# A hybrid decoder block on one core: compressed-branch probabilities stacked, gate weights as one stationary, fewer products for sums

## The chip, the cores and the metric

The kernel runs on one core of one Trainium2 chip. The metric is the device time of one execution in microseconds; of several executions the median is taken. Work is issued to five engines, each with its own instruction queue: TensorE (PE in the profile; PEld is its weight load), VectorE (DVE), ScalarE (ACT), GpSimd (POOL) and SyncE (SP, which here only issues DMA transfers).

## The reference

One layer on x of 256 rows by 1024 columns, with 256 memory rows. All inputs and outputs are fp32. Cut to the parts around the change:

```python
h = rmsnorm(x, g_pre_mix)
z = h @ w_in            # q, six k/v, gates, mLSTM inputs, q_mem, merge gates
# compressed branch: blocks of 32 rows, stride 16 -> 15 compressed keys and values
kc, vc = compress_blocks(k, ...), compress_blocks(v, ...)
s = einsum('bsghd,bngd->bghsn', q, kc) * NSA_SCALE
p = masked_softmax(s, end <= t)
o_cmp = einsum('bghsn,bngd->bsghd', p, vc)
# selected and window branches have the same q; with 256 rows both are causal softmaxes
gb = sigmoid(g_nsa)     # three gates a head: 48 columns of z
y_nsa = gb0 * o_cmp + gb1 * o_slc + gb2 * o_win
# mLSTM: 4 + 4 gate columns of z, a running sum of log-sigmoid over the rows, a running maximum
b = cumsum(logf); m_t = running maximum; ...
# memory cross-attention, merge of three projections, w_out, SwiGLU feed-forward of 2816
```

There are 4 groups of 4 query heads of 64 columns. rmsnorm needs the sum of squares of each row of x and of mem.

## The kernel before

**Precision.** A product of fp32 matrices is made of products of high and low parts: `split(hi, lo, src)` copies src to a rounded type on ACT (`hi`), and VectorE subtracts (`lo = src - hi`). A full product is hi·hi + lo·hi + hi·lo (`mm3`, `fmaj`, `tmaj`): three TensorE instructions for each 128-row step of the contraction. Weights come from HBM as units of 128 x 1024 (512 KB): the tile `raw` (four buffers) is filled by a DMA, `whi` (ACT) and `wlo` (VectorE) are made of it, four buffers each. Small products, such as sums by a column of ones, run in plain fp32.

**Stages.** First the keys and values of the memory: `memt` (mem, transposed, in pieces of two or one 128-row blocks) is scaled to `mh`, `ml`, and multiplied with the units of `mem_k` (0 to 3, the first three fetched in halves) and `mem_v`, while `xt` (x transposed, two DMAs of 512 KB) arrives. The sums of squares go through `colsum`: a product of the squares with a column of ones, one for each of two row halves `j` and two column halves `tb`. POOL raises them to the power -0.5, `bcast` spreads them, and VectorE and ACT make `xt` scaled, `hh` and `hl` (the parts of h).

Then the k/v units for the compressed branch ("kv" 0 to 3): `pd` goes to `st` (ACT and VectorE copies), `ph` is the first layer of the compression (32 products of 75 columns in fp32, two blocks of 16), `hid` its result. `w1` (two transfers of 1 MB) reuses the buffers of `memt`, `mh`, `ml`. `mraw` (masks, 208 KB) is issued behind it and cast to `msk`. The gates (`pgf`) are 56 columns of w_in: the host pads them to 128 columns (`wg`), `gw` holds the parts, and `fmaj` makes 8 x 3 products. `gts` is a copy, `pg` its transpose, `og` and `logf` follow. `pf` is the running sum (`tri` is a triangle of ones), `cm` the running maximum (eight VectorE steps on 4 x 256), `nm` its negative, `pm` brings it back to rows. `hrep` repeats the hidden values of the compressed v along the columns, so that the product `pvc` stands at every row block where it is wanted; `vcs` holds its high and low parts side by side (64 + 64 columns).

**Attention stage.** For 4 groups x 2 row halves, `nsa_half(g, tb, qs, yT)`: scores `sc`, maximum `mx`, exponentials `pp` (selected and window) and `pc` (compressed, 16 of 32 columns a head, the rest zero), scaled by the gates over the sums (`sm`). Then transposes `ptn` and `ptc`, parts `pTh`, `pTl` and `ch`, `cl`, and products into `pvn`, which holds the high part of v's columns on 64 partitions and the low part on the other 64. For the compressed branch the 128 rows of `ch` are 4 heads x 32; POOL multiplies with the mask `bm` to make `ce`, in which each head has its own 128 columns and zeros in the rows of the other heads, so that one stationary serves all heads. Other work (units of the mLSTM and of the merge gates) is called in between by `fill`.

Then projections, w_out, feed-forward.

**Order of instructions.** All operations are first recorded (`Plan.record`; hence nearly every row of the profile has the same line, L511, and tiles tell them apart). `Plan.choose` then lists them with a model of durations, dependences and buffers, tries variants of that list by a seeded random search, and issues the best in one fixed order per engine. Any change in an operation's size or number starts another search.

Of the kernel before, what the change touches and what calls it, by code (L numbers as in the profile page):

```python
# [11 lines left out]
F32 = mybir.dt.float32  # L12
# [502 lines left out]
def block_kernel(ctx, tc, order, xN, xT, memT, cst, vec, row, wg, w1, w2, W, out):  # L515
# [42 lines left out]
    def split(hi, lo, src):  # L558
        ACT.activation(hi, src, AF.Copy)
        DVE.tensor_sub(lo, src, hi.bitcast(F32))  # L560
# [95 lines left out]
    def colsum(sq):  # L656

        col = ps_t([P, 2], "col")
        for j in range(2):
            for tb in range(2):  # L660
                PE.matmul(col[:, tb:tb + 1], sq[:, j, tb * P:(tb + 1) * P], ones[:, 0:1],
                          start=j == 0 and tb == 0, stop=j == 1, skip_group_check=True)
        return col

    def bcast(r, ps):
# [35 lines left out]
        split(kmem[:, 0, 2 * i:2 * i + 2, :], kmem[:, 1, 2 * i:2 * i + 2, :], kt)  # L701

    rw = one.tile([P, 520], F32, name="rw")
    wgt = work.tile([P, 1024], F32, tag="p", bufs=2, name="wgt")
    w2t = one.tile([P, 192], F32, name="w2t")
    dma(out=vc, in_=vec)
    warm_up(10)
# [104 lines left out]


    pgf = ps_s([P, S], "pgf")
    gw = [wpool.tile([P, 1024], F32R, tag=t, bufs=4, name="gw") for t in ("whi", "wlo")]
    split(gw[0], gw[1], wgt)
    fmaj(pgf, X, range(KD), gw)
    gts = work.tile([64, S], F32, tag="sq", bufs=3, name="gts")
    DVE.tensor_copy(gts, pgf[0:64])
    pg = ps_s([P, 2, 64], "pg")  # L820
    for tb in range(2):
        PE.transpose(pg[:, tb, :], gts[:, tb * P:(tb + 1) * P], cs[0:64, K_ID:K_ID + 64])
# [15 lines left out]

    tri = cs[:, K_TRI:K_TRI + P]
    pf = ps_t([P, 2, 4], "pf")  # L840
    PE.matmul(pf[:, 0, :], tri, logf[:, 0, :], start=True, stop=True)
    PE.matmul(pf[:, 1, :], ones, logf[:, 0, :], start=True, stop=False)
    PE.matmul(pf[:, 1, :], tri, logf[:, 1, :], start=False, stop=True)
    Fs = one.tile([P, 2, 4], F32, name="Fs")
    DVE.tensor_copy(Fs, pf)
    As = one.tile([P, 2, 4], F32, name="As")
# [21 lines left out]
    DVE.tensor_add(idr, ident[:, 0:4], ident[:, 32:36])  # L868
    pm = ps_t([P, 2, 4], "pm")
    for tb in range(2):  # L870
        PE.matmul(pm[:, tb, :], nm[:, tb * P:(tb + 1) * P], cs[0:4, K_ID:K_ID + 4], start=True, stop=True)
    nmf = work.tile([P, 2, 4], F32, tag="g4", bufs=4, name="nmf")
    DVE.tensor_sub(nmf, pm, Fs)
    em = one.tile([P, 2, 4], F32, name="em")
# [9 lines left out]
    PE.matmul(pk, w2t[:, 0:P], hid[:, 0, :, 0:16], start=True, stop=True)  # L884
    split(kh[:, :, 256:272], kl[:, :, 256:272], pk)
    pvc = ps_t([P, NG, 64], "pvc")
    hrep = work.tile([P, NG, 4, 32], F32, tag="sq", bufs=3, name="hrep")
    POOL.tensor_tensor(hrep, hid[:, 1, :, :].unsqueeze(2).to_broadcast([P, NG, 4, 32]),
                       ones[:, 0:32].unsqueeze(1).unsqueeze(1).to_broadcast([P, NG, 4, 32]), op=ALU.mult)
    for g in range(NG):  # L890
        PE.matmul(pvc[:, g, :], hrep[:, g, :, :], w2t[:, P:192], start=True, stop=True)
    split(vcs[:, :, 0:64], vcs[:, :, 64:128], pvc)
# [188 lines left out]
    ynh = bigt("Y", 2, [P, 8, S], F32R, "ynh")  # L1081
    ynl = bigt("Y", 2, [P, 8, S], F32R, "ynl")
    exps = []
    pcs = [one.tile([P, HPG, 32], F32, name=f"pc{i}") for i in range(2)]
    for t in pcs:
        POOL.memset(t, 0.0)
    bm = cs[:, K_BM:K_BM + 4]
    rvalid = cs[:, K_RV:K_RV + 1]

    def nsa_half(g, tb, qs, yT):  # L1090
        t = slice(tb * P, (tb + 1) * P)
        pc = pcs[tb]
        pv = ps_v([P, HPG, P], "pvn")
        nkb = tb + 1
        for pr in range(2):
            mx = work.tile([P, 2, 3], F32, tag="mx", bufs=3, name="mx")
            sm = work.tile([P, 2, 3], F32, tag="sm", bufs=3, name="sm")
            pp = work.tile([P, 1024], F32, tag="p", bufs=2, name="pp")
            pv4 = pp[:, 0:512 * nkb].rearrange("p (h b n) -> p h b n", h=2, b=2)
            for j in range(2):  # L1100
                q = qs[:, 2 * pr + j, t]
                if tb == 0:
                    s = ps_s([P, 512], "sc")
                    PE.matmul(s[:, 0:272], q, kh[:, g, P:400], start=True, stop=False)
                    PE.matmul(s[:, 0:272], q, kl[:, g, P:400], start=False, stop=False)
                    PE.matmul(s[:, 0:272], identb, M0, start=False, stop=True)
                    sc = (s[:, P:144], s[:, 0:P], s[:, 144:272])
                else:
                    s, s2 = ps_s([P, 512], "sc"), ps_s([P, 512], "sc")
                    for x, c, n in ((s, 0, 272), (s2, 272, 256)):  # L1110
                        PE.matmul(x[:, 0:n], q, kh[:, g, c:c + n], start=True, stop=False, skip_group_check=True)
                        PE.matmul(x[:, 0:n], q, kl[:, g, c:c + n], start=False, stop=False, skip_group_check=True)
                    PE.matmul(s[:, 0:P], identb, MD, start=False, stop=False, skip_group_check=True)
                    PE.matmul(s[:, 256:272], identb, MC1, start=False, stop=True, skip_group_check=True)
                    PE.matmul(s2[:, P:256], identb, MD, start=False, stop=True, skip_group_check=True)
                    sc = (s[:, 256:272], s[:, 0:256], s2[:, 0:256])
                for b in range(3):
                    DVE.tensor_reduce(mx[:, j, b:b + 1], sc[b], axis=AX.X, op=ALU.max, negate=True)
                for b in range(3):
                    out = pc[:, 2 * pr + j, 0:16] if b == 0 else pv4[:, j, b - 1]  # L1120
                    exps.append(ACT.activation(out, sc[b], AF.Exp, bias=mx[:, j, b:b + 1],
                                               accum_out=sm[:, j, b:b + 1]))
            h0 = HPG * g + 2 * pr
            DVE.tensor_mul(sm, sm, og[:, tb, 3 * h0:3 * h0 + 6].rearrange("p (h b) -> p h b", h=2))
            DVE.reciprocal(sm, sm)
            if tb == 0:
                DVE.tensor_scalar(sm[:, :, 0], sm[:, :, 0], rvalid, None, op0=ALU.mult)
            for j in range(2):
                for b in range(3):
                    o = pc[:, 2 * pr + j, 0:16] if b == 0 else pv4[:, j, b - 1]  # L1130
                    DVE.tensor_scalar(o, o, sm[:, j, b:b + 1], None, op0=ALU.mult)
            for kb in range(nkb):
                pt = ps_t([P, 2, 2, P], "ptn")
                for b in range(2):
                    for j in range(2):
                        n = kb if b or not tb else 1 - kb
                        PE.transpose(pt[:, b, j, :], pv4[:, j, b, n * P:(n + 1) * P], ident)
                th = work.tile([P, 512], F32R, tag="pT0", bufs=2, name="pTh")
                tl = work.tile([P, 512], F32R, tag="pT1", bufs=2, name="pTl")
                split(th, tl, pt.rearrange("p a b c -> p (a b c)"))  # L1140
                for b in range(2):
                    for i, x in enumerate((th, tl)):
                        PE.matmul(pv[:, 2 * pr:2 * pr + 2, :], vs[:, kb, b, g, :], x[:, 256 * b:256 * b + 256],
                                  start=(pr == 0 and kb == 0 and b == 0 and i == 0), stop=False,
                                  skip_group_check=True)
        pt = ps_t([P, P], "ptc")
        PE.transpose(pt, pc.rearrange("p h n -> p (h n)"), ident)
        cl = work.tile([P, P], F32, tag="cl", bufs=1, name="cl")
        ch = work.tile([P, P], F32R, tag="ch", bufs=1, name="ch")
        ACT.activation(ch, pt, AF.Copy)  # L1150
        DVE.tensor_sub(cl, pt, ch.bitcast(F32))
        ce = [work.tile([P, HPG, P], F32R, tag=f"ce{i}", bufs=1, name=f"ce{i}") for i in range(2)]
        for i, x in enumerate((ch.bitcast(F32), cl)):
            POOL.tensor_tensor(ce[i], x.unsqueeze(1).to_broadcast([P, HPG, P]),
                               bm.unsqueeze(2).to_broadcast([P, HPG, P]), op=ALU.mult)
        for pr in range(2):
            for i in range(2):
                PE.matmul(pv[:, 2 * pr:2 * pr + 2, :], vcs[:, g, :], ce[i][:, 2 * pr:2 * pr + 2, :],
                          start=False, stop=(pr == 1 and i == 1), skip_group_check=True)
        ylo = work.tile([64, HPG, P], F32, tag="sq", bufs=3, name="ylo")  # L1160
        ACT.activation(ylo, pv[64:128], AF.Copy)
        for e in range(2):
# [163 lines left out]
def _layout(inputs):  # L1326
# [10 lines left out]
    def blocks(w, cols, k0=0, k1=None):  # L1337

        k1 = w.shape[0] // P if k1 is None else k1
        return w[k0 * P:k1 * P, cols].reshape(k1 - k0, P, -1).transpose(1, 0, 2)  # L1340
# [41 lines left out]
        pe("cmp_pe_k"), pe("cmp_pe_v")], axis=1)  # L1382
    w2 = np.concatenate([w2k, w2k, a["cmp_w2_v"][0]], axis=1)
    row = np.concatenate([a[n] for n in ("ml_head_g", "ml_gate_b", "g_post_mix", "g_post_ffn", "g_pre_ffn")], axis=1)
    wg = np.zeros((D, P), np.float32)
    wg[:, 0:48] = w_in[:, C_G:C_G + 48]
    wg[:, 48:56] = w_in[:, C_IF:C_IF + 8]
    wg = blocks(wg, slice(None)).reshape(P, 1024)

    cst = np.zeros((P, K_END), np.float32)  # L1390
    i = np.arange(P)
# [8 lines left out]
    cst[:, K_MT:K_MT + P] = np.where(i[:, None] <= i[None, :], 0.0, NEG)  # L1400
    cst[:, K_TRI:K_TRI + P] = i[:, None] <= i[None, :]
    cst[:, K_RV] = i >= 31
    cst[:, K_BM:K_BM + 4] = (i[:, None] // 32) == np.arange(4)[None, :]
    arrs = {"xN": a["x"][0], "xT": xT, "memT": memT, "cst": cst, "vec": vec, "row": row, "wg": wg, "w1": w1, "w2": w2}
    return {k: np.ascontiguousarray(v) for k, v in arrs.items()}, units

# [30 lines left out]
```

## Time and profile before

| what | value |
|---|---|
| median of 3 runs | 555.98 us (555.93, 555.98, 558.07) |
| profiled execution, span from first to last instruction | 558.1 us |
| TensorE busy | 545.3 us, 98% |
| VectorE busy | 422.2 us, 76% |
| ScalarE busy | 343.0 us, 61% |
| GpSimd busy | 31.7 us, 6% |
| mean granted TensorE clock | 0.992 |

The profiled execution's span agrees with the longest of the three runs (558.07). Busy time counts overlapping instructions once; TensorE's products overlap, so that a product lasts longer than the distance to the start of the next one. A row of a group of instructions reads: line, engine, operation, out<-in, shapes, xcount | busy us, mean ns | idle time before, and what ended it. A row of a timeline reads: start us, length us, engine, line, operation, tiles, shapes, count. An fp32 product shows as two records. In the rows the names are out<-moving,stationary for TensorE.

### The profile page before, as it was taken

How to read it: one execution, taken by the hardware profiler on the slowest of the kernel's cores; microseconds unless marked ns; L12 is line 12 of the kernel's file. 1: busy time of each engine (PE TensorE's matmuls, PEld its weight loads, DVE VectorE, ACT ScalarE, POOL GpSimd, SP SyncE). 2: the span in 40 equal slices, each digit the busy share in tenths (PEclk: the TensorE clock that was granted, in tenths of full speed). 3: DMA queues.
4: the chain of work that ended last, by engine and by line, in shares of the span. 5: the costliest groups of instructions: out<-in, count | busy, mean ns of one | idle time of the engine just before them, and what ended most of it. 6: DMA issues, size and time to landing. Idle time of an engine off the chain costs nothing.

```text
span 558.1 us, 8856 instructions
## 1 busy us (share of the span) xinstructions
PE 545.3 (98%) x3208; PEld 478.3 (86%) x3208; DVE 422.2 (76%) x811; ACT 343.0 (61%) x671; POOL 31.7 (6%) x44
## 2 busy tenths in 40 slices
PE   9998999999999999999999999999999999999995
PEld 8888999898989889889888888878888888888883
DVE  4885687679898988896896788884778787854543
ACT  6754667574688885776787444664566666643430
POOL 1100000001002122011101000000000000000000
PEclk9997999999999999999999999999999999999999
DMA  7894244743633164155354565652455555555512
GB/s 251 341 303 179 79 148 130 223 141 128 213 114 133 57 226 173 55 189 168 134 183 141 191 225 201 222 196 110 154 189 190 188 189 189 188 192 193 192 66 75
DMA packets 29419, 95.71 MB, mean 171 GB/s; under 512 B 3392, under 2 KB 6720, under 8 KB 29120
## 3 DMA queue, kind: packets, MB, share of 16 engines
q1 hardware_dynamic: 29376, 95.15, 49.1%
q8 instruction: 25, 0.41, 0.3%
q14 instruction: 18, 0.15, 0.1%
HBM read 93.04 MB, written 1.05 MB: 169 GB/s over the span
## 4 chain that ended last, share of the span: by engine, by line
PE 89%; DVE 6%; DMA 2%; issue 2%; ACT 1%; POOL 0%; SPq 0%; DVEq 0%; ACTq 0%
PE pd L511 47%; PE pss L511 28%; PE sc L511 3%; PE pvn L511 3%; PE ptn L511 2%; PE ph L511 2%; DVE wlo L511 2%; DMA memt<-in_memT 1%; DMA raw<-in_W 1%; PE pn L511 1%; DVE wq L511 1%; DVE xt L511 1%; DVE z L511 1%; DVE cm L511 1%; PE psm L511 1%
## 5 line engine op out<-in xcount | busy, mean ns | idle before, releaser
L511 DVE TENSOR_TENSOR wlo<-raw,whi 128x1024 fp32r<-128x1024 f32 (+1 forms) x161 | 193.8, 1209 | 69.1 <-ACT whi L511 65.2
L511 ACT ACTIVATE whi<-raw 128x1024 fp32r<-128x1024 f32 (+1 forms) x161 | 167.9, 1045 | 103.1 <-PE pd L511 56.1
L511 PE MATMUL pd<-hh,whi 128*128 128x256 f32 x224 | 65.2, 291 | 0.0
L511 PE MATMUL pd<-hh,wlo 128*128 128x256 f32 x224 | 64.4, 287 | 0.2 <-DVE wlo L511 0.2
L511 PE MATMUL pd<-hl,whi 128*128 128x256 f32 x224 | 64.3, 287 | 0.0
L511 PE MATMUL pd<-whi,hh 128*128 128x512 f32 x144 | 58.4, 407 | 0.0
L511 PE MATMUL pd<-wlo,hh 128*128 128x512 f32 x144 | 58.3, 405 | 0.0
L511 PE MATMUL pd<-whi,hl 128*128 128x512 f32 x144 | 57.3, 400 | 0.0
L511 PEld LDWEIGHTS pd<-hh,wlo 128*128 128x128 f32 x224 | 43.5, 194 | 0.4 <-DVE wlo L511 0.4
L511 PEld LDWEIGHTS pd<-hh,whi 128*128 128x128 f32 x224 | 43.6, 195 | 0.2
L511 PEld LDWEIGHTS pd<-hl,whi 128*128 128x128 f32 x224 | 43.5, 194 | 0.2
L511 PE MATMUL pss<-xc,whi 128*128 128x512 f32 x168 | 43.2, 392 | 0.0
L511 PE MATMUL pss<-whi,u 128*128 128x512 f32 x132 | 42.3, 392 | 0.0
L511 PEld LDWEIGHTS pss<-xc,whi 128*128 128x128 f32 x168 | 30.7, 189 | 5.4
L511 PE MATMUL pd<-xc,whi 128*128 128x512 f32 x120 | 31.9, 394 | 0.0
L511 PEld LDWEIGHTS pd<-whi,hh 128*128 128x128 f32 x144 | 27.2, 189 | 4.4
L511 PEld LDWEIGHTS pd<-whi,hl 128*128 128x128 f32 x144 | 27.2, 189 | 4.3
L511 PEld LDWEIGHTS pd<-wlo,hh 128*128 128x128 f32 x144 | 27.2, 189 | 4.1
L511 PEld LDWEIGHTS pss<-whi,u 128*128 128x128 f32 x132 | 24.8, 188 | 5.5
L511 ACT ACTIVATE pp<-sc,mx 128x128 f32<-128x128 f32 (+1 forms) x64 | 26.6, 430 | 2.8 <-DVE mx L511 2.7
L511 DVE TENSOR_REDUCE mx<-sc 128x1 f32<-128x16 f32 (+2 forms) x96 | 22.5, 289 | 5.0 <-PE sc L511 4.9
L511 PE MATMUL pss<-wlo,u 128*128 128x512 f32 x66 | 25.9, 392 | 0.0
(325 smaller groups left out, 1138.8 us busy)
## 6 DMA issues: line engine op xcount, KB each, us to landing
raw<-in_W SPq DMA_DIRECT2D x159, 512.0 KB, 3.3
w<-in_w SPq DMA_DIRECT2D x2, 1024.0 KB, 7.7
raw<-in_W SPq DMA_DIRECT2D x6, 256.0 KB, 4.9
xt<-in_xT SPq DMA_DIRECT2D x2, 512.0 KB, 7.0
kk<-kk SPq DMA_DIRECT2D x8, 128.0 KB, 3.0
x<-in_xN SPq DMA_DIRECT2D x2, 512.0 KB, 4.5
out<-z SPq DMA_DIRECT2D x8, 128.0 KB, 2.0
memt<-in_memT SPq DMA_DIRECT2D x6, 128.0 KB, 4.2
```

What stands on the lines that cost most here:

```text
L511: op.ins_ = getattr(op.real, op.method)(*map(arg, op.a), **{k: arg(x) for k, x in op.kw.items()})
```

## The change

1. `colsum`: VectorE adds the two halves `j` first, so that two products remain of four. It is called twice (mem, x).
2. Gates: the host packs 64 columns in place of 128; high and low parts stand side by side in one stationary of 128 columns (`gw`, one tile in place of two). Eight products give hi·hi and lo·hi on two halves of the partitions, eight more (64 columns) add hi·lo; ACT copies the second half, VectorE adds the first. 16 products in place of 24, one ACT instruction more.
3. `pf`: one product with `tri` for both halves, then one with ones: two in place of three. `pm`: two transposes in place of two products.
4. `hrep` repeats 8 x 16 in place of 4 x 32.
5. `nsa_half`: the scaled compressed probabilities are written twice (`pd`, 2 x 4 heads x 16). After the transpose rows 0 to 63 are kept as high part and rows 64 to 127 become the low part, in one tile `ch`. One masking by POOL (`ce`, two buffers) in place of two, and one product of 512 columns in place of four of 256.

Cut to its core:

```diff
     def colsum(sq):
-        for j in range(2):
-            for tb in range(2):
-                PE.matmul(col[:, tb:tb + 1], sq[:, j, tb * P:(tb + 1) * P], ones[:, 0:1],
-                          start=j == 0 and tb == 0, stop=j == 1, skip_group_check=True)
+        DVE.tensor_add(sq[:, 0, :], sq[:, 0, :], sq[:, 1, :])
+        for tb in range(2):
+            PE.matmul(col[:, tb:tb + 1], sq[:, 0, tb * P:(tb + 1) * P], ones[:, 0:1],
+                      start=tb == 0, stop=tb == 1, skip_group_check=True)
...
-    wgt = work.tile([P, 1024], F32, tag="p", bufs=2, name="wgt")
+    wgt = work.tile([P, 8, 64], F32, tag="p", bufs=2, name="wgt")
...
-    gw = [wpool.tile([P, 1024], F32R, tag=t, bufs=4, name="gw") for t in ("whi", "wlo")]
-    split(gw[0], gw[1], wgt)
-    fmaj(pgf, X, range(KD), gw)
+    gw = wpool.tile([P, 8, P], F32R, tag="whi", bufs=4, name="gw")
+    split(gw[:, :, 0:64], gw[:, :, 64:P], wgt)
+    for k in range(KD):
+        PE.matmul(pgf, gw[:, k, :], X[0][:, k, :], start=k == 0, stop=False, skip_group_check=True)
+    for k in range(KD):
+        PE.matmul(pgf[0:64], gw[:, k, 0:64], X[1][:, k, :], start=False, stop=k == KD - 1, skip_group_check=True)
-    DVE.tensor_copy(gts, pgf[0:64])
+    ACT.activation(gts, pgf[64:P], AF.Copy)
+    DVE.tensor_add(gts, gts, pgf[0:64])
...
-    PE.matmul(pf[:, 0, :], tri, logf[:, 0, :], start=True, stop=True)
-    PE.matmul(pf[:, 1, :], ones, logf[:, 0, :], start=True, stop=False)
-    PE.matmul(pf[:, 1, :], tri, logf[:, 1, :], start=False, stop=True)
+    PE.matmul(pf, tri, logf, start=True, stop=False, skip_group_check=True)
+    PE.matmul(pf[:, 1, :], ones, logf[:, 0, :], start=False, stop=True, skip_group_check=True)
...
-        PE.matmul(pm[:, tb, :], nm[:, tb * P:(tb + 1) * P], cs[0:4, K_ID:K_ID + 4], start=True, stop=True)
+        PE.transpose(pm[:, tb, :], nm[:, tb * P:(tb + 1) * P], cs[0:4, K_ID:K_ID + 4])
...
-    pcs = [one.tile([P, HPG, 32], F32, name=f"pc{i}") for i in range(2)]
-    for t in pcs:
-        POOL.memset(t, 0.0)
+    pcs = [one.tile([P, HPG, 16], F32, name=f"pc{i}") for i in range(2)]
+    pds = [one.tile([P, 2, HPG, 16], F32, name=f"pd{i}") for i in range(2)]
...
-                    o = pc[:, 2 * pr + j, 0:16] if b == 0 else pv4[:, j, b - 1]
-                    DVE.tensor_scalar(o, o, sm[:, j, b:b + 1], None, op0=ALU.mult)
+                    if b == 0:
+                        i = pc[:, 2 * pr + j, :].unsqueeze(1).to_broadcast([P, 2, 16])
+                        o = pd[:, :, 2 * pr + j, :]
+                    else:
+                        i = o = pv4[:, j, b - 1]
+                    DVE.tensor_scalar(o, i, sm[:, j, b:b + 1], None, op0=ALU.mult)
...
-        PE.transpose(pt, pc.rearrange("p h n -> p (h n)"), ident)
-        cl = work.tile([P, P], F32, tag="cl", bufs=1, name="cl")
-        ch = work.tile([P, P], F32R, tag="ch", bufs=1, name="ch")
+        PE.transpose(pt, pd.rearrange("p a h n -> p (a h n)"), ident)
+        ch = work.tile([P, P], F32R, tag="ch", bufs=2, name="ch")
         ACT.activation(ch, pt, AF.Copy)
-        DVE.tensor_sub(cl, pt, ch.bitcast(F32))
-        ce = [work.tile([P, HPG, P], F32R, tag=f"ce{i}", bufs=1, name=f"ce{i}") for i in range(2)]
-        for i, x in enumerate((ch.bitcast(F32), cl)):
-            POOL.tensor_tensor(ce[i], x.unsqueeze(1).to_broadcast([P, HPG, P]),
-                               bm.unsqueeze(2).to_broadcast([P, HPG, P]), op=ALU.mult)
-        for pr in range(2):
-            for i in range(2):
-                PE.matmul(pv[:, 2 * pr:2 * pr + 2, :], vcs[:, g, :], ce[i][:, 2 * pr:2 * pr + 2, :],
-                          start=False, stop=(pr == 1 and i == 1), skip_group_check=True)
+        DVE.tensor_sub(ch[64:128], pt[64:128], ch[64:128].bitcast(F32))
+        ce = work.tile([P, HPG, P], F32R, tag="ce", bufs=2, name="ce")
+        POOL.tensor_tensor(ce, ch.bitcast(F32).unsqueeze(1).to_broadcast([P, HPG, P]),
+                           bm.unsqueeze(2).to_broadcast([P, HPG, P]), op=ALU.mult)
+        PE.matmul(pv, vcs[:, g, :], ce, start=False, stop=True, skip_group_check=True)
```

The search makes another order of it, on every engine up to the end of the attention stage; after it TensorE's order is the old one. Three places follow.

SP's queue at the start of the program, before: `memt` is the memory, `raw` the weight units (128x512 is half a unit of `mem_k` 0 to 2, 128x1024 a whole one, first that of `mem_k` 3), `xt` is x.

```order
L511 DMA memt<-in_memT 128x256
L511 DMA raw<-in_W 128x512
L511 DMA memt<-in_memT 128x512
L511 DMA raw<-in_W 128x1024 x3
L511 DMA xt<-in_xT 128x1024 x2
L511 DMA cs<-in_cst 128x128
```

And in the changed kernel:

```order
L511 DMA memt<-in_memT 128x256
L511 DMA raw<-in_W 128x512
L511 DMA xt<-in_xT 128x1024
L511 DMA memt<-in_memT 128x512
L511 DMA raw<-in_W 128x1024 x3
L511 DMA xt<-in_xT 128x1024
```

Half of `xt` stands ahead of the last piece of `memt` and of the unit of `mem_k` 3. Moreover the two first half units stand ahead of the first piece of `memt`, and the unit that was fetched ahead of `wgt` now stands between the two transfers of `w1`.

TensorE's queue at the first `ph`, the compression's first layer, before (`pd<-hh` and `pd<-hl` are products of h with k/v weights):

```order
L511 MATMUL pd<-hh,wlo 128x256
L511 MATMUL pd<-hh,whi 128x256
L511 MATMUL pd<-hl,whi 128x256
L511 MATMUL pd<-hh,wlo 128x256
L511 MATMUL ph<-st_95,w_0_424 128x75 x16
```

And in the changed kernel:

```order
L511 MATMUL pd<-hh,wlo 128x256
L511 MATMUL pd<-hh,whi 128x256
L511 MATMUL pd<-hl,whi 128x256
L511 MATMUL ph<-st_84,w_0_381 128x75 x16
L511 MATMUL pd<-hh,wlo 128x256
```

Two products, of unit 3's high part, have moved ahead of `ph`.

TensorE's queue in the first half of the attention stage, before: from the last product with the exponentials (`pTl`) to the end of the half; `pd<-whi,hh` is filling work with 512 columns.

```order
L511 MATMUL pvn<-pTl,vs 128x256
L511 MATMUL pvn<-ce_1519,vcs 128x256
L511 MATMUL pd<-wlo,hh 128x512
L511 MATMUL pd<-whi,hl 128x512
L511 MATMUL pd<-whi,hh 128x512
L511 MATMUL pd<-wlo,hh 128x512
L511 MATMUL pd<-whi,hl 128x512
L511 MATMUL pd<-whi,hh 128x512
L511 MATMUL pvn<-ce_1540,vcs 128x256
L511 MATMUL pvn<-ce_1519,vcs 128x256
L511 MATMUL pvn<-ce_1540,vcs 128x256
```

And in the changed kernel:

```order
L511 MATMUL pvn<-pTl,vs 128x256
L511 MATMUL pd<-whi,hh 128x512
L511 MATMUL pd<-wlo,hh 128x512
L511 MATMUL pd<-whi,hl 128x512
L511 MATMUL pd<-whi,hh 128x512
L511 MATMUL pd<-wlo,hh 128x512
L511 MATMUL pvn<-ce,vcs 128x512
```

The four products with the compressed probabilities, spread over two places, have become one. Between the transpose `ptc` and the first of them stand 18 products before and 19 now.

More of the change, by code (lines that the diff above doesn't have):

```diff
@@ L886, in block_kernel @@
     pvc = ps_t([P, NG, 64], "pvc")
-    hrep = work.tile([P, NG, 4, 32], F32, tag="sq", bufs=3, name="hrep")
-    POOL.tensor_tensor(hrep, hid[:, 1, :, :].unsqueeze(2).to_broadcast([P, NG, 4, 32]),
-                       ones[:, 0:32].unsqueeze(1).unsqueeze(1).to_broadcast([P, NG, 4, 32]), op=ALU.mult)
+    hrep = work.tile([P, NG, 8, 16], F32, tag="sq", bufs=3, name="hrep")
+    POOL.tensor_tensor(hrep, hid[:, 1, :, 0:16].unsqueeze(2).to_broadcast([P, NG, 8, 16]),
+                       ones[:, 0:16].unsqueeze(1).unsqueeze(1).to_broadcast([P, NG, 8, 16]), op=ALU.mult)
     for g in range(NG):
@@ L1091, in nsa_half @@
         t = slice(tb * P, (tb + 1) * P)
-        pc = pcs[tb]
+        pc, pd = pcs[tb], pds[tb]
         pv = ps_v([P, HPG, P], "pvn")
@@ L1119, in nsa_half @@
                 for b in range(3):
-                    out = pc[:, 2 * pr + j, 0:16] if b == 0 else pv4[:, j, b - 1]
+                    out = pc[:, 2 * pr + j, :] if b == 0 else pv4[:, j, b - 1]
                     exps.append(ACT.activation(out, sc[b], AF.Exp, bias=mx[:, j, b:b + 1],
@@ L1384, in _layout @@
     row = np.concatenate([a[n] for n in ("ml_head_g", "ml_gate_b", "g_post_mix", "g_post_ffn", "g_pre_ffn")], axis=1)
-    wg = np.zeros((D, P), np.float32)
+    wg = np.zeros((D, 64), np.float32)
     wg[:, 0:48] = w_in[:, C_G:C_G + 48]
     wg[:, 48:56] = w_in[:, C_IF:C_IF + 8]
-    wg = blocks(wg, slice(None)).reshape(P, 1024)
+    wg = np.ascontiguousarray(blocks(wg, slice(None)))
     cst = np.zeros((P, K_END), np.float32)
@@ L1402, in _layout @@
     cst[:, K_RV] = i >= 31
-    cst[:, K_BM:K_BM + 4] = (i[:, None] // 32) == np.arange(4)[None, :]
+    cst[:, K_BM:K_BM + 4] = (i[:, None] % 64 // 16) == np.arange(4)[None, :]
     arrs = {"xN": a["x"][0], "xT": xT, "memT": memT, "cst": cst, "vec": vec, "row": row, "wg": wg, "w1": w1, "w2": w2}
```

## The prediction

> **What bounds the kernel now.** I read the page first, then the list of PE's waits, then the chain of waits for start-to-start times, then the timeline around each place that the change touches. The page's rows:
>
> ```profile
> span 558.1 us, 8856 instructions
> PE 545.3 (98%) x3208; PEld 478.3 (86%) x3208; DVE 422.2 (76%) x811; ACT 343.0 (61%) x671; POOL 31.7 (6%) x44
> DVE  4885687679898988896896788884778787854543
> ```
>
> PE is the bound nearly everywhere; VectorE (DVE, in tenths of 40 slices) comes near it in the attention stage, slices 8 to 24. PE's waits (engine, tile, releaser, us in total, times, longest) are few:
>
> ```profile
> PE ph L511 <- DVE st L511: 2.0, 1, 2.0
> PE pm L511 <- DVE nm L511: 0.4, 1, 0.4
> PE pvn L511 <- POOL ce L511: 0.4, 1, 0.4
> ```
>
> So a product taken off PE should be worth its start-to-start time, not its duration: products overlap. The chain gives that time, as start, length, count:
>
> ```profile
> 54.98 2.88 PE pgf L511 x24
> 298.70 8.31 PE pss L511 x36
> ```
>
> A product with 256 moving columns costs 2.88/24 = 0.12 us, one with 512 costs 8.31/36 = 0.231 us. The mean durations of the groups (near 0.28 and 0.39) would overstate every saving.
>
> **The parts, one by one.** (1) Last products of a half of the sparse attention (eight halves). Four products of 256 columns become one of 512.
>
> ```profile
> L511 PE MATMUL pvn<-ce,vcs 128*128 128x256 f32 x32 | 6.5, 284 | 0.4 <-POOL ce L511 0.4
> 129.23 0.52 PE L511 MATMUL pvn<-ce,vcs 128*128 128x256 f32 x3
> 129.58 0.65 PE L511 MATMUL sc<-kk,qs 128*128 128x272 f32 x4
> ```
>
> Three of them take 129.58 - 129.23 = 0.35, so 0.117 each. Per half 4 x 0.117 = 0.47 goes and 0.231 comes: -0.24, times 8 = -1.9 us. The bounds of a single half are 0 (if PE then waits for another engine) and -0.35 (if the new one cost no more than an old one); I take the middle one because its 512 columns have a row. Each of the 32 small scalings now writes 32 columns in place of 16 (0.23 us at 16 columns, 0.28 at 128 by the rows below); 16 more columns add about 0.01 each, 0.3 us of VectorE over the whole stage, hidden by PE's queue.
>
> ```profile
> L511 DVE TENSOR_SCALAR pc<-pc,sm 128x16 f32<-128x16 f32 x32 | 7.3, 228 | 0.2
> L511 DVE TENSOR_SCALAR pp<-pp,sm 128x128 f32<-128x128 f32 x32 | 8.3, 281 | 0.0
> L511 POOL TENSOR_TENSOR ce<-cl,cs 128x512 fp32r<-128x512 f32 x8 | 9.5, 1187 | 0.0
> ```
>
> The second masking on GpSimd, 1.19 us a half, goes too. Alone that is worth nothing on an engine that is busy 6%. But it stood between the transpose and the last products, and once PE waited for it:
>
> ```profile
> 172.07 0.28 PE L511 MATMUL pd<-hl,whi 128*128 128x256 f32 x1
> 172.73 0.62 PE L511 MATMUL pvn<-ce,vcs 128*128 128x256 f32 x3 [0.38 <-POOL ce L511]
> ```
>
> Start to start 0.66 instead of 0.12: 0.54 us lost. The chain is now 1.19 shorter, and in the new order PE has more products between the transpose and the last one (19 after 18 in the first half). I count -0.54, bounds 0 and -0.54.
>
> (2) Gate weights: 24 products of 256 columns become 16, -8 x 0.12 = -0.96. Half of the new ones have 64 stationary columns; I give them no discount, since 256 columns move all the same. The split of the weights halves, and the sum of the two halves costs one more instruction on ACT, ahead of one on VectorE in place of the old copy; 64-row copies of that width take about 0.4 us on VectorE (row 43.03 below, four in 1.63), and I take the same for ACT. Cover: before the transposes pg stand 17 products of the next unit, 2.0 us, where there were 9. If they did not cover it, 0.4 us came back.
>
> (3) Column sums: two calls, each with two products fewer and one 128x256 add more.
>
> ```profile
> L511 DVE TENSOR_TENSOR join<-join 128x256 f32<-128x256 f32 x18 | 7.7, 426 | 0.6
> 20.60 0.39 PE L511 MATMUL pss<-whi,mh 128*128 128x512 f32 x1
> 20.83 0.28 PE L511 MATMUL col<-ones,msq 128*128 128x1 f32 x2
> 20.97 0.48 PE L511 MATMUL pss<-wlo,mh 128*128 128x512 f32 x1
> 21.28 0.28 PE L511 MATMUL col<-ones,msq 128*128 128x1 f32 x2
> 24.04 0.95 PE L511 MATMUL col<-ones,sq 128*128 128x1 f32 x8
> 24.85 0.69 PE L511 MATMUL rbc<-cs,rm 128*128 128x128 f32 x4
> ```
>
> An fp32 product shows as two records. From 20.60 to 21.28 are two big products and one small: 0.68 - 2 x 0.231 = 0.22. From 24.04 to 24.85 are four: 0.20 each. Four fewer: -0.84. The adds (0.43 each, by the first row) lengthen VectorE's chain to hl by up to 0.85. PE then meets hl late in the first kv unit, but it has 2 us of waiting ahead of it anyway, at ph (below), which covers that; without that cover it costs 0.85.
>
> (4) Prefix sums: three products become two. Two transposes replace two products at pm.
>
> ```profile
> 63.51 0.28 PE L511 MATMUL pf<-logf,cs 128*128 128x4 f32 x2
> 64.10 0.36 PE L511 MATMUL pd<-hl,whi 128*128 128x256 f32 x1
> 73.48 0.57 PE L511 MATMUL pm<-cs,nm 4*128 4x4 f32 x4 [0.43 <-DVE nm L511]
> 73.98 0.43 PE L511 MATMUL pk<-hid,w2t 128*128 128x64 f32 x2
> 88.14 1.04 PE L511 MATMUL ptx<-cs,pp 128*128 128x128 f32 x8
> 88.93 0.36 PE L511 MATMUL pd<-hh,wlo 128*128 128x256 f32 x1
> ```
>
> pf: 0.59/3 = 0.2 saved. pm: 0.50 for two becomes two transposes at 0.79/8 = 0.1, 0.3 saved. Together -0.5. The wait for nm (0.43) I leave: in the new order the scan has one more weight split between its steps (about 1.2 us) and PE nine more products ahead of pm (1.1 us). The hrep edit keeps the sizes: 0. The memsets of pc that vanish are GpSimd's, busy 6%: 0.
>
> (5) What the planner moved. Every length changes, so the order is searched anew, and SP's queue changes at the start: half of xt (512 KB) is now issued ahead of the last piece of memt and of the weights of unit 3 of mem_k. There the DMA engines have no room, and PE is waiting (windows: us, busy per engine, clock, DMA share, GB/s):
>
> ```profile
> 6.00:8.00 2.00, 1.98 (x15) 1.66 (x14) 0.86 (x3) 1.03 (x2) 0.00 (x0) 1.00 0.88 236
> 8.00:10.00 2.00, 2.00 (x15) 1.79 (x15) 1.47 (x4) 1.73 (x3) 0.00 (x0) 1.00 0.99 306
> 14.00:16.00 2.00, 1.62 (x15) 1.42 (x13) 1.54 (x3) 2.00 (x4) 0.00 (x0) 1.00 1.03 420
> 13.13 0.91 ACT L511 ACTIVATE mh<-memt,vc 128x256 fp32r<-128x256 f32 x2 [0.36 <-DMA memt<-in_memT]
> 14.89 1.99 ACT L511 ACTIVATE whi<-raw 128x1024 fp32r<-128x1024 f32 x2
> 16.16 1.22 DVE L511 TENSOR_TENSOR wlo<-raw,whi 128x1024 fp32r<-128x1024 f32 x1
> 17.43 0.39 PE L511 MATMUL pd<-mh,wlo 128*128 128x256 f32 x1 [0.70 <-DVE wlo L511]
> ```
>
> ACT takes memt as soon as it lands (13.13), then squares, then splits the weights; VectorE follows and PE starts on wlo at 17.43. From there PE is busy without a gap until mem_v ends. 0.524 MB at 420 GB/s is 1.25 us, at 306 it is 1.7. All of that chain moves back. I take +1.3, since the nearer row is that of 14 us; bounds 0 (the transfer slips into the share left free before 8 us) and 1.9 (with the first products 0.2 later, as memt is issued third).
>
> What comes after: the first ph.
>
> ```profile
> 42.63 0.38 DVE L511 CAST msk<-mraw 128x416 bf16<-128x416 f32 x1 [2.23 <-DMA mraw<-in_cst]
> 43.03 1.63 DVE L511 COPY st<-pd 64x255 f32<-64x255 f32 x4
> mraw<-in_cst SPq DMA_DIRECT2D x1, 208.0 KB, 8.6
> 46.90:53.70 6.80, 6.80 (x34) 6.80 (x33) 2.92 (x4) 2.54 (x3) 0.00 (x0) 0.50 0.69 231
> ```
>
> VectorE stands at the cast for mraw, with the copies that ph needs behind it. mraw is issued behind the second w1, which takes a buffer of mh or ml and so is issued when mem_v's products are done. So ph moves with that end: 1.3 - 0.84 = +0.46, and the stall stays about 2 us. In the new order two products of the next unit stand ahead of ph and need the transfer after mraw; they only change places, 0, with +0.5 as the upper bound. Sum: -1.9 - 0.54 - 0.96 - 0.84 - 0.5 = -4.74 taken away, +1.3 given back: -3.4 us. Against the profiled execution (span 558.1, which is also the time of the longest of the three runs) that is 554.7; against the median of 555.98 it is 552.6, and 0.5% of it, 2.8 us, is about what a measurement can tell from no change.
>
> **The clock, and the rivals.** The last row above shows a granted clock of 0.50 for 6.8 us: it begins some 2 us after the copies that ph waits for, so PE's wait of 2.0 us and then ph's 75-column products lie before it. Its price is at most half of 6.8, 3.4 us, and the two runs that are 2.1 us shorter than the third may be runs without it (not shown). Rival one: the start trips it too. PE stands idle there for 0.38 us between 14 and 16 and for 0.70 before 17.43; with 1.3 more it is 2.4, and dense products follow: 6.8 us at half clock cost 3.4. With the 1.3 this leaves -4.74 + 4.7 = 0.0, 556.0; with 1.9 it ends at +0.6, 556.5, slower than before. It decides at a loss at the start of 4.74 us, and is slower by over 0.5% only above 7.5. For it: the row shows such a drop after a stop of 2 us. Against it: in the profile the stops before 17.43 had no drop (clock 1.00 in the rows to 16), and a few products still break the new one. [...] I give it 0.15, of which 0.09 ends slower by over 0.5% or near it with other losses.
>
> Rival two: the transfer of xt is hidden (it fits before 8 us, where the share is 0.88): -4.74, 551.2. Chance 0.13. Rival three: in the attention stage VectorE (76% over the span, 8 or 9 tenths there) sets the pace and its new order eats what PE saves there, so -4.74 + 2.44 + 1.3 = -1.0, 555.0. For it: those tenths; against it: the list of waits has one of PE in that stage, the one for ce. Chance 0.17. My forecast, -2.8 to -4.2, has 0.55.
>
> **How the numbers follow.** Faster by over 0.5% (below 553.2): most of the forecast (0.45) and rival two (0.13), 0.58. Within 0.5%: the rest of the forecast, rival three, part of rival one, 0.33. Slower: 0.09. The range goes from 550.5, rival two with the last products near their bound of -0.35 a half, to 556.5, rival one's upper end; the forecast's own is 551.8 to 553.3.
>
> **What would show it.** Right: pgf 16 products at 0.12; 8 products of 512 columns at 0.23 and no wait for ce; the first wlo products of unit 3 near 18.8; ph's start near 45.5 with a wait near 2 us. Wrong: a clock of 0.50 before 30 us, first wlo of unit 3 still near 17.4, or new waits of PE for VectorE after 100 us.

## The result

The changed kernel takes 552.94 us, median of five executions (551.44 to 553.59), against 555.98 for the kernel before (555.73 to 558.75). The ratio is 0.9933, with a 95% interval of 0.9911 to 0.9955: 3 us faster. Forecast were 552.6, between 550.5 and 556.5. In both kernels an execution may or may not contain stretches of half TensorE clock (the mean clocks of the executions on record are 0.989 to 0.999 before and 0.993 to 0.997 in the changed kernel's five), and the profiled execution of before has such a stretch (0.50 from 46.90 to 53.70). In the runs on record the time is 1.7 to 2.0 us longer than the span, mostly 1.8, so its span of 558.1 stands for a time near 559.9 and not for the run of 558.07, as the note under the table of before and the prediction have it; the median of 555.98 has a span of 554.2. The differences of single rows below are therefore taken place by place.

The page of the changed kernel, first the rows that answer to those shown of before:

```profile
span 551.1 us, 8728 instructions
PE 539.2 (98%) x3164; PEld 472.0 (86%) x3164; DVE 422.5 (77%) x813; ACT 342.7 (62%) x672; POOL 20.5 (4%) x34
```

Then the list of PE's waits (releaser, us in total, times, longest):

```profile
PE pd L511 <- ACT mh L511: 1.1, 1, 1.1
PE pd L511 <- ACT whi L511: 1.1, 1, 1.1
PE pd L511 <- DVE wlo L511: 0.7, 1, 0.7
PE ph L511 <- issue: 0.3, 1, 0.3
```

The waits at pm for nm (0.4) and at pvn for ce (0.4) are gone, and the one at ph (2.0) is down to 0.3. The list puts the rest to "issue", but ph still starts just behind the copies to `st` (shown below: they end at 45.41, ph starts at 45.51). At the start the list of before has:

```profile
PE pd L511 <- DVE wlo L511: 0.9, 2, 0.7
PE pd L511 <- ACT whi L511: 0.4, 1, 0.4
```

The waits for mh and for unit 3's whi have grown; that for its wlo (0.7) is as long as before.

The chain of waits and the timeline (start, length) at the products that the change replaced:

```profile
52.53 1.88 PE pgf L511 x16
125.67 0.39 PE L511 MATMUL pvn<-ce,vcs 128*128 128x512 f32 x1
125.89 0.39 PE L511 MATMUL pd<-whi,hl 128*128 128x512 f32 x1
71.84 0.28 PE L511 MATMUL pm<-cs,nm 4*128 4x4 f32 x2
72.05 0.43 PE L511 MATMUL pk<-hid,w2t 128*128 128x64 f32 x2
```

16 gate products take 1.88, 0.1175 each, those with 64 stationary columns included; the new last product takes 125.89 - 125.67 = 0.22; two transposes at pm take 0.21, with no wait ahead.

At the start, timeline of PE and ACT, and windows (us, busy time of PE, PEld, DVE, ACT, POOL with counts, clock, DMA share, GB/s):

```profile
14.12 0.91 ACT L511 ACTIVATE mh<-memt,vc 128x256 fp32r<-128x256 f32 x2 [1.91 <-DMA memt<-in_memT]
15.64 0.28 PE L511 MATMUL pd<-mh,wlo 128*128 128x256 f32 x1
16.98 0.39 PE L511 MATMUL pd<-mh,whi 128*128 128x256 f32 x1 [1.06 <-ACT whi L511]
18.43 0.39 PE L511 MATMUL pd<-mh,wlo 128*128 128x256 f32 x1 [0.71 <-DVE wlo L511]
15.60:19.00 3.40, 1.63 (x11) 1.22 (x10) 2.99 (x4) 2.27 (x3) 0.00 (x0) 1.00 0.98 388
19.10:22.40 3.30, 3.30 (x18) 3.30 (x17) 3.08 (x6) 2.70 (x4) 0.00 (x0) 0.50 0.87 256
```

The last piece of memt reaches ACT at 14.12 instead of 13.13 and the first low product of unit 3 starts at 18.43 instead of 17.43. PE is busy for 1.63 of 3.40 us there, and the next 3.4 us run at a clock of 0.50, with 18 products in 3.3 us.

Last, ph:

```profile
42.36 0.37 DVE L511 CAST msk<-mraw 128x416 bf16<-128x416 f32 x1
43.68 1.73 DVE L511 COPY st<-pd 64x255 f32<-64x255 f32 x4 [0.87 <-ACT st L511]
44.89 0.28 PE L511 MATMUL pd<-hl,whi 128*128 128x256 f32 x1
45.51 4.38 PE L511 MATMUL ph<-st,w 128*128 128x75 f32 x32 [0.34 <-issue]
49.63 0.39 PE L511 MATMUL pd<-hh,wlo 128*128 128x256 f32 x1
```

The cast no longer waits for mraw; the copies wait for ACT's copies of the same pd. ph starts at 45.51, but PE's last product ahead of it also starts later, at 44.89 (42.67 before), and ph's 16 products take 49.63 - 45.51 = 4.12 us at full clock (50.42 - 44.92 = 5.50 before, mostly at half).

### The profile page after: what moved, and what is told of

Its sections match the earlier page's. It is cut to its first block, busy times and chain, and to the rows that moved or that the text cites. A ratio compares the mean times of both kernels' runs of the same rounds, so it can differ in the third digit from the quotient of the medians.

```text
span 551.1 us, 8728 instructions
## 1 busy us (share of the span) xinstructions
PE 539.2 (98%) x3164; PEld 472.0 (86%) x3164; DVE 422.5 (77%) x813; ACT 342.7 (62%) x672; POOL 20.5 (4%) x34
## 4 chain that ended last, share of the span: by engine, by line
PE 92%; DVE 3%; DMA 2%; issue 1%; ACT 1%; SPq 0%; DVEq 0%; ACTq 0%
PE pd L511 49%; PE pss L511 29%; PE sc L511 3%; PE pvn L511 2%; PE ptn L511 2%; PE ph L511 2%; DMA memt<-in_memT 1%; DMA raw<-in_W 1%; DVE wlo L511 1%; PE pn L511 1%; DVE wq L511 1%; PE psm L511 1%; DVE z L511 1%; PE pvm L511 1%; PE pq L511 1%
```

## The experiments

All order edits below are made after the planner's search, so that every engine keeps its order but for what is named. They were measured later, partly on other chips, each beside the kernel before, whose median was 556.46, 556.30 and 556.66 there after 555.98. So a difference of less than half a us between an experiment and the changed kernel shows nothing.

**Where half of xt stands.** `xt_late` moves the first half back behind the units:

```diff
+x0, x1 = [o for o in sp if name(o) == "xt"]
+move(x0, x1)
```

> The changed kernel with one transfer moved in SyncE's queue: the first half of xt is issued behind the units, next to the second half, as before the change; all else stands in the same order. Theory (the transfer ahead of memt costs PE its length at the start, and the long wait there also brings a window of half clock): the last piece of memt lands near 13.1 instead of 14.1 us, the first low products of mem_k's unit 3 start near 17.4 instead of 18.4, no granted clock of 0.50 before 30 us; 1.0 from the wait and about 1.5 from the clock, 550.4 us after 552.9. Rival one (the clock falls by chance of place, not by this wait): the window stays, 551.9. Rival two (the start has slack behind it: hl or mem_v's units wait instead): 552.9, with a new wait of PE between 20 and 45 us.

Measured: 550.77 (550.53 to 552.68), 0.9881 of before, interval 0.9846 to 0.9916; 2.2 less than the changed kernel. No version measured is faster, but for `xt_memt` below, which holds the same move.

```profile
13.16 0.91 ACT L511 ACTIVATE mh<-memt,vc 128x256 fp32r<-128x256 f32 x2 [0.56 <-DMA memt<-in_memT]
17.21 0.28 PE L511 MATMUL pd<-ml,whi 128*128 128x256 f32 x1
17.46 0.39 PE L511 MATMUL pd<-mh,wlo 128*128 128x256 f32 x1
15.60:19.00 3.40, 3.40 (x28) 3.22 (x28) 3.40 (x4) 2.40 (x3) 0.00 (x0) 1.00 1.03 408
19.10:22.40 3.30, 3.30 (x22) 2.96 (x21) 3.17 (x8) 2.50 (x5) 0.00 (x0) 1.00 0.92 328
```

memt is there 0.96 earlier, the low product starts at 17.46, PE has no wait in that stretch and the clock stays at 1.00. In these two profiles the low product moved by 1.0 and the first product of the k/v units by 2.5 (35.36 to 32.88), and 2.3 of it are left at the end of the span. One profile is a sample, though: with xt late, in this order, the low product starts at 16.88, 17.46, 17.46, 17.88 and 17.93 in five profiles (mean 17.5), with xt early at 18.28 and 18.43. The next run takes transfer and clock apart.

`busy_start` leaves the transfers and gives PE something to do in the wait:

```diff
+for i in (late, lo):
+    n = order.index(pe[i])
+    order[n:n] = [warm] * 2
```

> The changed kernel with four further warming products of 128 columns (two ahead of the first product of mem_k's unit 3, two ahead of its first low product), which write a tile that nobody reads; no transfer is moved. They fill some 0.9 of 1.2 us and 0.9 of 0.9 us in which PE waits. Theory (idle time of PE in a window brings the half clock, and the window of 3.4 us costs about 1.5): the waits' ends stay at 17.0 and 18.4, no granted clock of 0.50 after them, 551.4 us. Rival (the clock falls for another reason, or the window costs nothing because PE waits behind it anyway): 552.9, or 553.1 with the further products.

Measured: 551.50 (551.33 to 551.96).

```profile
17.40 0.60 PE L511 MATMUL warm<-ones 128*128 128x128 f32 x4
18.28 0.39 PE L511 MATMUL pd<-mh,wlo 128*128 128x256 f32 x1 [0.27 <-DVE wlo L511]
15.60:19.00 3.40, 2.19 (x17) 1.81 (x16) 3.14 (x4) 3.19 (x4) 0.00 (x0) 1.00 0.99 392
19.10:22.40 3.30, 3.30 (x24) 3.00 (x23) 3.19 (x7) 1.80 (x4) 0.00 (x0) 1.00 0.87 258
```

The low product starts at 18.28, hardly earlier, PE is busy 2.19 in place of 1.63, and the half clock is gone: four products that compute nothing bring 1.4 us. All six executions lie within 0.7 us, while four of the changed kernel's five lie at 552.8 to 553.6 and the fifth at 551.44, with a mean clock of 0.997 (the profiles without the window have 0.996 to 0.998, the two of this order with one 0.994). So the window costs about 1.4 us, it comes from PE's idle time, and of the 2.2 us about 0.7 to 0.8 are left for the transfer itself.

The two stretches compared do not begin and end where the clock changed, however. In the changed kernel's trace the half clock lasts from 19.06 to 22.47 and sets in again at 548.12; in that of before it lasts from 46.90 to 53.72 and sets in again at 555.48. So it lasted one and two times 3.413 us, and from its end to the next drop it was 154 and 147 times 3.413 us. Counted in such steps from the changes in its own profile, one window of the changed kernel goes from 15.64 to 19.06 and holds both waits; in `busy_start`, windows go from 14.56 to 17.97 and on to 21.38. By these windows:

| profile | window | PE busy in it, us | clock of the next window |
|---|---|---|---|
| `after_seed2` (below) | 14.15 to 17.57 | 1.32 | 0.50 |
| changed kernel | 15.64 to 19.06 | 1.65 | 0.50 |
| `xt_memt` (below) | 4.54 to 7.95 | 1.89 | 0.50 |
| `after_seed1` (below) | 13.58 to 16.99 | 2.00 | 1.00 |
| `before_seed2` (below) | 14.70 to 18.12 | 2.16 | 1.00 |
| changed kernel | 5.40 to 8.82 | 2.26 | 1.00 |
| `busy_start` | 14.56 to 17.97 | 2.48 | 1.00 |

Without its four products the window of `busy_start` would have held about 1.6 us of work (3.41 less the waits of 1.38 and 0.41 in it; an estimate).

`xt_memt` also moves the first piece of memt to the head of the queue:

```diff
+move(next(o for o in sp if name(o) == "memt"), sp[0])
```

> The changed kernel with the first half of xt moved behind the units as in the run before, and the first piece of memt moved to the head of SyncE's queue. Theory (the end of the first stage is set by the landing of memt's last piece and of unit 3, not by when PE begins): the first products start near 5.3 instead of 6.7 us, and the 1.4 us come back as a longer wait before unit 3; the same time as without this move, 550.4, or up to 1.5 more if that longer wait brings a half clock. Rival (the late first product costs what it shows, 1.4 us): 549.0.

Measured: 550.66 (550.50 to 551.97), no difference from 550.77. But the first product did not move, so the rival was not tried:

```profile
6.11 0.91 ACT L511 ACTIVATE mh<-memt,vc 128x256 fp32r<-128x256 f32 x2 [0.81 <-DMA vc<-in_vec]
6.67 0.51 PE L511 MATMUL pd<-mh,whi 128*128 128x256 f32 x2 [1.50 <-ACT mh L511]
7.95:11.30 3.35, 3.35 (x18) 3.35 (x18) 2.29 (x5) 2.88 (x6) 0.00 (x0) 0.50 0.91 258
```

mh also needs vc, which still stands behind two half units; I had overlooked it. What the late first product costs stays open. In this profiled execution (551.97, the longest of the six) the wait of 1.5 us ahead of 6.67 lies within one window of the clock, and the next is at half.

**The stall at ph in the kernel before.** `mraw_early`, made from before:

```diff
+w1 = next(o for o in sp if name(o) == "w1_1")
+move(next(o for o in sp if name(o) == "mraw"), w1)
```

> The kernel before the change with one transfer moved in SyncE's queue: mraw is issued ahead of the second w1 instead of behind it. Theory (the stall at ph in the kernel before came from mraw's cast, and the half clock of two windows from that stall): the cast runs before 41 us, the copies to st begin when ACT's are done, near 41.7, ph starts near 43.6 instead of 44.9, no half clock of 6.8 us after it; 1.3 from the wait and 1.5 to 3.0 from the clock, so 552 to 553 us after 556.0. Rival (VectorE's copies wait for something else, or the second w1, 0.5 us later, holds up the second ph): no more than 0.5 us gained, 555.5.

Measured: 555.84 (555.50 to 556.51), 0.9971, interval 0.9948 to 0.9994. The steps came as the theory had them:

```profile
40.56 0.37 DVE L511 CAST msk<-mraw 128x416 bf16<-128x416 f32 x1
41.97 1.63 DVE L511 COPY st<-pd 64x255 f32<-64x255 f32 x4 [1.03 <-ACT st L511]
46.90:53.70 6.80, 6.80 (x58) 6.80 (x57) 4.04 (x8) 2.97 (x5) 0.00 (x0) 1.00 0.61 199
```

The gain did not: 0.6 of the median, where 3 to 4 were expected. All twelve executions lie at spans of 553.7 to 554.7. Of the seventeen of before beside them, ten lie at 553.9 to 554.8 with a mean clock of 0.996 to 0.998, and seven at 556.3 to 559.3 with 0.989 to 0.995. So the half clock is in some executions of before only, the profiled one among them; the edit takes it out of all twelve, which is worth 1.8 us of the mean (557.6 to 555.9) but little of the median. `before_again` is the kernel before, unedited, to see one of the others:

> The kernel before the change, once more, for a second profile: its runs beside the last experiments lay between 553.9 and 559.3 us of span, and the run with mraw early at 553.7 to 554.7 throughout. Theory (when mraw lands decides between them): in an execution near 554.3 mraw lands early enough for a wait at ph of about 0.8 us, with no half clock behind it; in one near 558 the wait is near 2 us and the half clock is there. Rival (the clock alone makes the difference): a wait near 2 us at ph and no half clock in an execution near 554.3.

Measured: 556.88, span 555.1.

```profile
PE col L511 <- DVE sq L511: 0.9, 1, 0.9
PE ph L511 <- DVE st L511: 0.7, 1, 0.7
PE pm L511 <- DVE nm L511: 0.4, 1, 0.4
PE pvn L511 <- POOL ce L511: 0.4, 1, 0.4
42.36 0.38 DVE L511 CAST msk<-mraw 128x416 bf16<-128x416 f32 x1 [0.97 <-DMA mraw<-in_cst]
44.66 4.38 PE L511 MATMUL ph<-st,w 128*128 128x75 f32 x32 [0.70 <-DVE st L511]
46.90:53.70 6.80, 6.80 (x58) 6.80 (x57) 4.36 (x8) 3.35 (x4) 0.00 (x0) 1.00 0.73 231
```

The wait is 0.7 and there is no half clock, but mraw is hardly earlier (the cast starts at 42.36 after 42.63); PE is later, by a wait of 0.9 at col. The theory was half right: in both profiles ph's start is tied to mraw, and what differs is how long PE has to stand there (start to start 2.25 and 0.99). Two profiles do not tell how often which wait occurs, and none is of a median execution. The waits at pm and ce are in this execution too; the one at col is not in the first.

These windows hold ph's 75-column products, and there the busy time tells less: before a half clock PE was busy for 1.98 us (first profile of before, 43.48 to 46.90), 2.24 (`before_seed2`) and 2.68 (`after_seed2`), before a full one for 2.71 (`before_again`, 42.74 to 46.16). The drop came here behind 2.24 and 2.68, and at the start it did not come behind 2.16; what makes the difference was not tried.

**Are the products worth their start-to-start time?** From `xt_late`, with the products put back:

```diff
+for op in [o for o in order if o.eng == "PE" and o.kw.get("start")]:
+    again(op, {"pvn": 2, "pgf": 8, "col": 2, "pf": 2}.get(name(op), 0))
```

> The changed kernel with xt late (550.8 us), the order kept, and TensorE's products that the change took away put back as repeats of a group's first product, which starts its sum and so may stand several times without changing a value: 2 of 256 columns in each of the 8 halves of the attention (four of 256 cost as much as one of 512 and two of 256), 8 at the gates, 2 at each of the two column sums, 2 at the running sum. Theory (each product is on the path and is worth its start-to-start time): 16 x 0.12 + 8 x 0.12 + 4 x 0.2 + 2 x 0.2 = 4.1 us more, 554.9. Rival (VectorE or a transfer sets the pace in the attention stage or at the start, so part of the products is free): 552.9 or less.

Measured: 554.91 (554.66 to 557.60), 4.14 more than `xt_late`. And `nsa_back`, with "pvn" alone:

> As the run beside it, with only the 16 products of the attention stage put back. Theory: 16 x 0.12 = 1.9 us more than 550.8, 552.7. Rival (VectorE bounds the attention stage, rival three of the prediction): 550.8 to 551.4.

Measured: 552.36 (552.21 to 552.82), 1.6 more, 0.10 for each of 16 products. The whole is the theory's to the tenth; the attention stage's share is a little less and the rest, 2.55 for 2.2, a little more. Part of that is the start again: in the profile of `products_back` the low product of unit 3 comes 0.5 later than in `xt_late`'s, and place by place its products cost 0.9 at col, 1.0 at the gates, 0.45 at pf and 1.8 in the attention stage, 4.1 together. Rival three (VectorE sets the pace there) is excluded. Not put back are the two products at pm, for which the second repeat at pf stands, and nothing is taken off VectorE.

**The second masking.** `mask_twice`, from `xt_late`:

```diff
+for op in [o for o in order if o.eng == "POOL" and name(o) == "ce"]:
+    again(op, 1)
```

> The changed kernel with xt late (550.8 us), the order kept, and each of the 8 maskings by GpSimd issued twice, one behind the other, with the same result. In the changed kernel the last product of a half starts 0.52 to 0.73 us after the masking ends. Theory (the change shortened the chain and its new order spent the cover on something else, so the shorter chain is now needed): a second masking of 1.04 us makes PE wait about 0.5 us in each of the eight halves, 4 us more, 554.8. Rival (the masking was idle work off the path, as the page's 6% for GpSimd suggests): no more than 0.5 us, 551.3 at most.

Measured: 557.98 (557.06 to 560.16), 7.2 more, slower than the kernel before. List of waits, timeline of POOL and PE at two halves:

```profile
PE pvn L511 <- POOL ce L511: 4.9, 8, 1.3
121.02 2.23 POOL L511 TENSOR_TENSOR ce<-ch,cs 128x512 fp32r<-128x512 f32 x2 [51.52 <-DVE ch L511]
162.94 3.02 POOL L511 TENSOR_TENSOR ce<-ch,cs 128x512 fp32r<-128x512 f32 x2 [18.12 <-DVE ch L511]
122.57 0.39 PE L511 MATMUL pd<-wlo,hh 128*128 128x512 f32 x1
123.30 0.50 PE L511 MATMUL pvn<-ce,vcs 128*128 128x512 f32 x1 [0.34 <-POOL ce L511]
```

PE waits in each of the eight halves. Two maskings take 2.23 us here, 3.02 in the next half; PE's gap ahead of the product is 0.73 start to start here and 1.60 there. Over the eight halves the gap ahead of the product and the time from it to the next start are 10.3 us together, after 3.35 in `xt_late`: 7.0 of the 7.2, where the theory had 4. In the changed kernel GpSimd is busy 4% of the time and PE never waits for its masking; one microsecond more a half puts it on the path eight times, because the new order starts the last product 0.52 to 0.73 us behind the end of the masking.

**Is it a lucky order?** The search was started with 1 and 2 in place of 0, in both kernels (`rng = random.Random(1)`):

> The kernel before the change with another start of the random search (1 in place of 0), so that the same work stands in another order up to the end of the attention stage. Theory (most of the change's gain is work taken from TensorE, whatever the order): within 1.5 us of the kernel before, 555 to 558, and above both orders of the changed kernel. Rival (the gain is a lucky order): it spreads by 3 us or more, and reaches 553.

> As the run beside it, with start 2. Theory: 555 to 558. Rival: spread by 3 us or more among the orders of the kernel before, one of them near 553.

> The changed kernel with start 1 of the search. Theory (4.7 us of work and waits are gone in every order, and an order gives back at the start what xt's place costs, 0 to 2.5 us with the clock): 550 to 553. Rival (the gain is a lucky order): 553 to 556, among the orders of the kernel before.

> The changed kernel with start 2 of the search. Theory: 550 to 553. Rival: 553 to 556.

| start of the search | before | changed |
|---|---|---|
| 0 | 555.98 | 552.94, 0.9933 of before (0.9911 to 0.9955) |
| 1 | 555.72, 0.9976 of before (0.9958 to 0.9994) | 551.76, 0.9909 (0.9881 to 0.9938) |
| 2 | 556.91, 1.0010 (0.9980 to 1.0041) | 553.50, 0.9934 (0.9908 to 0.9960) |

The three orders of a kernel spread by 1.2 and 1.7 us; the means differ by 556.20 - 552.73 = 3.5, and every changed one is below every one of before. So the gain is the change's and not the draw's; but which draw one gets moves the result by half of what the change brings, and start 2 of the changed kernel lies 0.5 above the 550 to 553 expected. `xt_late` is below all of them.

The two further orders of the changed kernel have the transfers at the start as before the change, xt behind the units. That does not make them safe: the profile of start 2 (557.63, the slowest of its ten) has the last piece of memt at 14.63, the low product at 18.93 and half clock behind it. What xt's place costs is therefore shown for the order of start 0 alone.

## Why the prediction was right, and where by luck

**Products: right.** -1.9 - 0.96 - 0.84 - 0.5 = -4.2 were forecast, and putting them back costs 4.14 (with two at pf in place of one there and two at pm). The gate products with 64 stationary columns cost the same as the others, as assumed.

**The wait for ce: right.** It stands in both profiles of before and is gone. `mask_twice` shows more: the shorter chain would be worth much more than 0.54 in an order that counts on it.

**The price of xt's place: the size right, a part missing.** The low product of unit 3 moved by 0.8 to 1.0 (forecast 1.3, from the transfer's size at 420 GB/s). But rival one came true in part: the start did trip the half clock, for one window instead of two, at 1.4 us. It was given 0.15 and a price of 3.4, with 4.7 in all as its point of decision; it came with a stop that left PE idle for 1.8 of 3.4 us. The argument against it, that "a few products still break the new one", failed. In the traces one stretch of half clock at 19.1 to 22.4 came behind a window with 1.65 us of PE's work in 3.41, and one of 6.8 us at 46.90 to 53.70 in the profile of before behind one with 1.98.

**pm: missed.** The wait for nm, which I left in the sum, is gone: -0.58 (0.70 start to start in the second profile of before, 0.12 for a product without a wait; the changed kernel's profile has 0.21 there, which makes it -0.49).

**ph: the start right by luck, the reason wrong.** ph starts at 45.51, forecast 45.5, but the wait is 0.5 and not 2: PE comes to it 2.2 us later than before and waits 1.6 less, and these two nearly make the +0.46 of the sum. The step that failed is "So ph moves with that end" with a stall that "stays about 2 us": ph no longer waits for mraw. The unit that now stands between the two w1 had stood ahead of the first one and held it up; the text on the change names the move, the prediction only the queue, and no term of the sum prices it. The first w1 was issued 2.8 us earlier (24.18 after 26.95), took 8.2 us and was through when the second was issued (35.32); before, it took 8.6 and was not (33.68). The DMA traffic between 33.3 and 36 us, first of before, then of the changed kernel:

```profile
DMA packets 97, 0.66 MB, mean 246 GB/s; under 512 B 16, under 2 KB 16, under 8 KB 16
DMA packets 1, 0.00 MB, mean 0 GB/s; under 512 B 1, under 2 KB 1, under 8 KB 1
```

So the second w1 and mraw, though issued 1.6 us later (mraw at 35.70 after 34.05), found the transfer engines free. mraw landed after 5.1 us in place of 8.6, at 40.8, before VectorE came to the cast at 42.36; with 8.6 the cast would have stood until 44.3, ph would have started at 46.6 by the rows of before (44.92 after 42.63), and PE would have waited 1.6 (an estimate). That this order owes it to the unit's move is read from the traces and not tested alone. Nor is the move needed: in the two other orders of the changed kernel that unit still stands ahead of both w1, mraw takes 7.1 and 7.2 us, and the cast does not wait for it either.

**The sum.** From the second profile of before, whose ph waits 0.7, and without its wait at col: products -4.14, ce -0.54, pm -0.58, ph -0.37 (0.99 start to start, now 0.62), start +1.0, clock +1.4, which is -3.2 against -3.04 measured; with the 0.7 to 0.8 that `busy_start` leaves for the transfer it is -3.5. The tenths are not settled, since that execution (556.88) is not a median one. My -3.4 was nearly the same because two omitted gains (pm and ph, 0.9) stood against an omitted loss (the clock, 1.4; "a clock of 0.50 before 30 us" was on my own list of what would show me wrong). Against the profiled execution the sum failed: 554.7 forecast, a span of 551.1 now, since most of the stall of 2.1 us and its two windows of half clock went as well. From ph to the first gate product the two profiles of before differ by 2.8 us (9.90 and 7.08), which is the price of the two windows, so the 3.4 of the prediction for them was near the top. They are not in the median of before, so against that the same sum held.

## What to carry to other kernels

Price a removed TensorE product by its start-to-start time, and trust that price where the list of waits is empty: 30 products put back cost 4.14 us for 4.1 forecast. Read what a new search does to the transfer queue at the start as carefully as the change itself: in this order one 512 KB transfer in the wrong place cost 2.2 of the 5.2 us that the change could bring. And before a sum is made from one profiled execution, look whether its long waits are in the other executions too.

## What the runs showed of the hardware

While PE had work, the half clock came in the profiles of the two kernels in stretches of 3.41 us (19.06 to 22.47, the changed kernel) and 6.83 us (46.90 to 53.72, before). Among the windows of dense products in the table, those with 1.32, 1.65 and 1.89 us of PE's work in 3.41 were followed by a half clock, those with 2.00 and more were not. The two waits of the start share a window in the changed kernel's profile (15.64 to 19.06) and not in that of `busy_start` (14.56 to 17.97 and on to 21.38); that this place varies fits that the drop does not come in every execution of the same kernel (one of the changed kernel's five had a mean clock of 0.997 and a span of 549.6, the others 0.993 to 0.994 and 551.0 to 551.8), but a single profile per order cannot show it. The one window at the start cost about 1.4 us (552.94 after 551.50 in `busy_start`), and the four products that compute nothing, put into the waits there, left the clock at 1.00. GpSimd's masking of 128x512 took 1.04 us in six halves of the changed kernel and 2.08 in two (minimum, median, maximum in ns):

```profile
L511 POOL TENSOR_TENSOR ce<-ch,cs x8: 1042/1044/2082, 123.9 to 291.4; 128x512 fp32r<-128x512 f32 x8
```

What stretched it was not tried.
